# Strassen's block product for the gate and up tiles of two SwiGLU layers

## The chip, the cores and the metric

The kernel runs on one core of one Trainium2 chip, as one program from the inputs in DRAM to the output in DRAM. The metric is the time of one execution in microseconds (us) on the device, the median of several runs. A core has these engines: TensorE (PE, with its weight loads shown apart as PEld), VectorE (DVE), ScalarE (ACT), GpSimd (POOL), and SyncE (SP), which here only issues DMAs.

## What is computed

Two transformer blocks on 512 tokens of width 1024. The first block has two layers: a gated delta rule or a forgetting attention as mixer, and after each mixer a SwiGLU feed-forward layer (FFN) with normed input and normed output:

```python
D_FF = 2816          # of width 1024: 22 tiles of 128

def swiglu(h, w_in, w_out):
    gu = h @ w_in
    return (jax.nn.silu(gu[..., :D_FF]) * gu[..., D_FF:]) @ w_out

for layer in range(2):
    ...                                   # mix: gated delta rule (0), forgetting attention (1)
    x = x + rms_norm(mix, post_mix_norm[layer])
    f = swiglu(rms_norm(x, pre_ffn_norm[layer]), w_ffn_in[layer], w_ffn_out[layer])
    x = x + rms_norm(f, post_ffn_norm[layer])
```

A second block with two other attentions follows. All of it is float32 in the reference, and the output must come close to float32.

## The kernel before

Activations lie transposed: 8 tiles of 128 features by 512 tokens. To keep close to float32, every operand of a big product is split into two float32r parts, `hi` (the rounded value) and `lo` (the rest), and a product of 128x128 weights by a stretch of tokens is three matmuls, hi·hi, hi·lo and lo·hi (`mm3`, L670). A unit of weights (`weight`, L686) is 128 x 1024, that is 8 blocks of 128x128: SP loads it from DRAM, ACT or DVE rounds it into `hi`, ACT or DVE writes `-hi` into `lo`, and a second DMA, issued by POOL, adds the DRAM values onto that (`lows`, L676).

There are five stages: gdn, ffn0, fox, ffn1, b2. An FFN (`ffn`, L883) has 22 pairs of a gate tile and an up tile. In `fm_phase` (L720) each tile of 128 output features is 8 blocks x 3 = 24 matmuls of 512 tokens into one PSUM bank. `evac_in` (L892) takes it out: DVE multiplies by the row norm `y.rb`, ACT and DVE form the SiLU of the gate, DVE or POOL multiplies the two, and the result is split into `hidden[j]`. `FF_CUT` cuts the 22 pairs into stretches of 7, 8 and 7: after each stretch the 8 output tiles are multiplied over its hidden tiles and added up in `f`. At the head of an FFN four tiles, and at its tail four output tiles, are done in two halves of 256 tokens (`HALVES`), so that the norm of one half of the tokens can run beside matmuls of the other. The norm and residual (`add_normed`, L787) come at the end of each mixer and each FFN, nearly all of it on DVE and ACT.

The order of all instructions is made beforehand by a planner (`Program.schedule`, L330). It goes through the recorded operations with a cost for each (`cost`, L258), five queues (PE, DVE, ACT, POOL, SP), and a priority that is the place in the program plus a shift (`SHIFTS`, `later`). Operations that several engines can do (`copy`: ACT or DVE; `tt`: DVE or POOL) go where they end first after a handicap (`DEAR`). `WINDOWS` bounds how far ahead it looks, `QUOTAS` how many weight tiles may be in use at once: 3 raw ones, 10 `hi` or `lo` parts. There are 57 `big` tiles (128 x 512), 21 `wide` ones (128 x 1024) and 8 PSUM banks. A list of engines whose operations exclude each other at a shared port is part of the plan (`locks`, L292). `x`, the residual, stays in 8 `big` tiles through an FFN.

Of the kernel before, what the change touches and what calls it, by code (L numbers as in the profile page):

```python
# [30 lines left out]
DEAR = {"gdn": {"DVE": 650, "ACT": 0, "POOL": 600},  # L31
        "ffn0": {"DVE": 800, "ACT": 0, "POOL": 1000},
        "fox": {"DVE": 850, "ACT": 150, "POOL": 750},
        "ffn1": {"DVE": 450, "ACT": 200, "POOL": 1000},
        "b2": {"DVE": 450, "ACT": -200, "POOL": 400}}
WINDOWS = {"gdn": 881, "ffn0": 1155, "fox": 774, "ffn1": 1400, "b2": 1181}
GDN_ORDER = ("K2 K0 K3 K1 P2 I0 P0 K4 D0 R0 D1 P1 R1 D3 P3 R3 D2 K5 K7 K6 I1 R2 P5 O0 D4 D5 D6 "
             "D7 P7 P4 P6 R4 R6 R5 R7")
FOX_ORDER = "K012 K4 V0 K6 H1 H2 K3 H3 H0 V1 K7 H4 K5 H6 H7 H5 O"
B2_ORDER = "B1 S3 B3 B2 S2 B0 S1 v k q o A1 A0 A2 A3"  # L40
SELECT_SHIFT = 943
START_SHIFT = 50
# [10 lines left out]
class View:  # L53
# [3 lines left out]
    def __init__(self, tile, dt, a, steps=()):  # L57
        self.tile, self.dt, self.a, self.steps = tile, dt, a, steps
# [5 lines left out]
    def __getitem__(self, key):  # L64
        return View(self.tile, self.dt, self.a[key], self.steps + (lambda r: r[key],))
# [475 lines left out]
                getattr(eng[o.eng], fn)(*(real(a) for a in args), **{k: real(a) for k, a in kw.items()})  # L541


class Normed:


    def __init__(self, net):
# [8 lines left out]
class Net:  # L556
# [277 lines left out]

    def out_proj(self, w, o, f, x, post, pre, dst):

        y = Normed(self)
        ws = sum((self.weight_pair(w, m, slice(512, 1024)) for m in range(0, KD, 2)), [])
        for cols in HALVES:
            acc = self.t(256)  # L840
            for m in range(KD):
                bank = self.bank()[:, :256]
                self.fm_tile(bank, ws[m], o, cols)
                self.V.tensor_add(f[m][:, cols], bank, f[m][:, cols])
                self.acc_sq(m, f[m][:, cols], acc)
            self.add_normed(cols, x, f, acc, post, y, pre, dst)
        return y
# [32 lines left out]
            self.block2(first("b2", "n2"), src)  # L880


    def ffn(self, layer, y, x, post, pre, dst):  # L883
        V, A, P = self.V, self.A, self.P
        w_in, w_out = self.d[f"w_ffn_in{layer}"], self.d[f"w_ffn_out{layer}"]
        f = [self.t() for _ in range(KD)]
        nxt = Normed(self)
# [1 line left out]
        gates = {}  # L889
        hidden = {}  # L890

        def evac_in(m, ps, cols):  # L892
            j, up = divmod(m, 2)
            w = cols.stop - cols.start
            if not up:
                gr, th = self.t(w), self.t(w)
                V.tensor_mul(gr, ps, y.rb[:, cols])
                A.activation(th, gr, AF.Tanh, scale=0.5)
                V.scalar_tensor_tensor(gr, th, 1.0, gr, op0=OP.add, op1=OP.mult)
                gates[j, cols.start] = gr  # L900
            else:
                gr = gates.pop((j, cols.start))
                ur = self.t(w)
                V.tensor_mul(ur, ps, y.rb[:, cols])
                self.tt(ur, gr, ur, OP.mult)
                if j not in hidden:
                    hidden[j] = self.t(T, F32R), self.t(T, F32R)
                self.split(hidden[j][0][:, cols], hidden[j][1][:, cols], ur, 0.5)

        j0 = 0  # L910
        for c, n in enumerate(FF_CUT):
            last = c == len(FF_CUT) - 1
            items = [(m, w_in[m]) for m in range(2 * j0, 2 * (j0 + n))]
            self.fm_phase(items, 1024, y.pairs(), evac_in, head=(c == 0))

            def evac_out(m, ps, cols):
                fm = f[m][:, cols]
# [12 lines left out]
            items = [(m, w_out[m][:, j0 * 128:(j0 + n) * 128]) for m in range(KD)]  # L930
# [425 lines left out]
    def fox(self, y, x, w_out):  # L1356
# [89 lines left out]

        for step in FOX_ORDER.split():
            if step[0] == "K":
# [424 lines left out]
```

## Time and profile before

| | us |
|---|---|
| median of 3 runs (1697.17 to 1701.31) | 1697.29 |
| the profiled execution, its own time | 1699.14 |
| its span, from the first to the last instruction | 1697.4 |
| PE busy in the span | 1660.2 |
| DVE, ACT, POOL busy in the span | 1043.3, 916.4, 425.2 |

The profile is of one execution. Busy time of PE is modelled, since matmuls overlap: the distance between starts in a long run of like matmuls tells its pace better than the duration of one (about 400 ns for 512 columns, where starts are some 230 ns apart). A few matmul records can be missing. "Idle before, releaser" says what ended an engine's idle time. All program instructions have line 541 (L541), the line in which the planned order is issued, so groups are told apart by tiles: `big<-psum,big` writes a big tile from a PSUM bank and a big tile, `wide` are weights, `s` small ones.

### The profile page before, as it was taken

The numbers are of one execution on the slowest core, as the hardware profiler recorded it, in microseconds if no ns is written. First come the engines' busy times: TensorE is split into PE (matmuls) and PEld (weight loads), VectorE is DVE, ScalarE is ACT, GpSimd is POOL, SyncE is SP. The second block draws the span as 40 slices with busy tenths as digits, with TensorE's granted clock in tenths as the row PEclk, the third lists the DMA queues.
The fourth block names the chain that finished last, engine by engine and source line by source line (L and its number), as shares of the span: only waits on it lengthen the run. The fifth ranks groups of instructions, "written<-read, shape, count | busy, mean of one in ns | idle before, by whom it ended". The sixth has DMA issues, their size and how long they took to land.

```text
span 1697.4 us, 24959 instructions
## 1 busy us (share of the span) xinstructions
PE 1660.2 (98%) x8886; PEld 1405.1 (83%) x8886; DVE 1043.3 (61%) x2607; ACT 916.4 (54%) x1847; POOL 425.2 (25%) x466
## 2 busy tenths in 40 slices
PE   7999999999999999999999999999999999999999
PEld 5888988997888888887888897888888889898787
DVE  7995875683313223385879684324324477999896
ACT  7643844564234524365978572122512377796694
POOL 3322423221201211122232221201311121413751
PEclk9999999999999999999999999999999999999999
DMA  9746568449967967667354659968958595538723
GB/s 264 161 100 175 101 143 209 119 123 223 214 163 187 222 163 176 158 190 196 88 113 114 161 133 220 229 171 192 231 144 185 132 233 147 126 64 216 170 69 87
DMA packets 105084, 276.24 MB, mean 163 GB/s; under 512 B 24160, under 2 KB 29024, under 8 KB 104960
## 3 DMA queue, kind: packets, MB, share of 16 engines
q0 software_dynamic: 37952, 124.83, 41.0%
q1 hardware_dynamic: 67008, 149.82, 25.7%
q8 instruction: 70, 1.15, 0.3%
q14 instruction: 54, 0.44, 0.1%
HBM read 266.68 MB, written 7.86 MB: 162 GB/s over the span
## 4 chain that ended last, share of the span: by engine, by line
PE 84%; DMA 6%; DVE 4%; issue 3%; POOL 2%; ACT 2%; SPq 0%; POOLq 0%; DVEq 0%; ACTq 0%
PE psum L541 84%; DVE big L541 3%; DMA wide<-in_w_ffn_in_dram 2%; DMA wide<-in_w_gdn_dram 1%; ACT big L541 1%; POOL big L541 1%; DMA wide<-in_gdn_w_out_dram 1%; DMA wide<-in_w_sm_dram 1%; DMA wide<-in_w_v_dram 1%; POOL s L541 1%; ACT wide L541 0%; POOL wide L541 0%; DMA big<-in_xT_dram 0%; DVE wide L541 0%; DMA s<-in_w_ba_dram 0%
## 5 line engine op out<-in xcount | busy, mean ns | idle before, releaser
L541 PE MATMUL psum<-big,wide 128*128 128x512 f32 (+1 forms) x5872 | 1279.8, 372 | 20.5 <-DMA wide<-in_w_gdn_dram 7.3
L541 PEld LDWEIGHTS psum<-big,wide 128*128 128x128 f32 x5872 | 1003.4, 189 | 212.6 <-DMA wide<-in_w_gdn_dram 8.4
L541 DVE TENSOR_TENSOR big<-psum,big 128x512 f32<-128x512 f32 (+5 forms) x334 | 186.4, 566 | 410.0 <-PE psum L541 390.1
L541 ACT ACTIVATE big<-big 128x256 f32<-128x256 f32 (+4 forms) x312 | 159.6, 524 | 458.8 <-DVE big L541 446.1
L541 PE MATMUL psum<-wide,big 128*128 128x512 f32 (+2 forms) x924 | 211.2, 374 | 1.8 <-DMA wide<-in_w_sm_dram 0.8
L541 ACT ACTIVATE wide<-wide 128x1024 fp32r<-128x1024 f32 (+4 forms) x180 | 181.8, 1031 | 23.6 <-PE psum L541 21.6
L541 PEld LDWEIGHTS psum<-wide,big 128*128 128x128 f32 x924 | 156.9, 188 | 29.4 <-DMA wide<-in_w_sm_dram 1.3
L541 POOL DMA_DIRECT2D wide<-in_w_ffn_in_dram x88 | 82.3, 987 | 388.7 <-ACT wide L541 339.2
L541 ACT CAST wide<-wide 128x1024 fp32r<-128x1024 f32 (+3 forms) x178 | 177.0, 1019 | 3.9 <-DMA wide<-in_gdn_w_out_dram 2.1
L541 DVE TENSOR_TENSOR big<-big,big 128x256 f32<-128x256 f32 (+3 forms) x315 | 161.9, 528 | 21.5 <-ACT big L541 17.4
L541 ACT COPY big<-psum 128x512 f32<-128x512 f32 (+3 forms) x128 | 71.7, 560 | 136.4 <-PE psum L541 134.8
L541 DVE SCALAR_TENSOR_TENSOR big<-big,big 128x512 f32<-128x512 f32 (+3 forms) x153 | 103.3, 678 | 65.7 <-ACT big L541 63.5
L541 ACT ACTIVATE big<-big,s 128x128 f32<-128x128 f32 (+3 forms) x266 | 135.5, 542 | 13.0 <-DVE s L541 11.9
L541 PE MATMUL psum<-big,big 128*128 128x128 f32 (+9 forms) x672 | 118.2, 303 | 2.3 <-ACT big L541 1.6
L541 POOL TENSOR_TENSOR s<-s,half 128x4 f32<-128x4 f32 (+2 forms) x50 | 63.4, 1295 | 202.7 <-DVE s L541 191.1
L541 PEld LDWEIGHTS psum<-big,big 128*128 128x128 f32 (+2 forms) x672 | 95.0, 190 | 8.9 <-issue 2.0
L541 PE MATMUL psum<-ident,big 128*128 128x128 f32 (+1 forms) x564 | 94.4, 272 | 4.8 <-DVE big L541 2.8
L541 POOL TENSOR_TENSOR big<-big,big 64x512 fp32r<-64x512 f32 (+3 forms) x56 | 69.8, 1257 | 112.6 <-DVE big L541 41.3
L541 POOL DMA_DIRECT2D wide<-in_w_ffn_out_dram x48 | 44.1, 1045 | 181.2 <-ACT wide L541 149.9
L541 PEld LDWEIGHTS psum<-ident,big 128*128 128x128 f32 (+1 forms) x564 | 68.9, 140 | 20.4 <-issue 4.3
L541 DVE SCALAR_TENSOR_TENSOR big<-big,gains,big 128x256 f32<-128x256 f32 (+2 forms) x144 | 71.8, 525 | 0.7 <-ACT big L541 0.6
L541 DVE CUSTOM_DVE_ANT_0 big<-psum,big 128x384 f32<-128x384 f32 (+3 forms) x120 | 57.3, 495 | 3.3 <-PE psum L541 2.8
(137 smaller groups left out, 1311.6 us busy)
## 6 DMA issues: line engine op xcount, KB each, us to landing
wide<-in_w_ffn_in_dram SPq DMA_DIRECT2D x88, 512.0 KB, 8.2
wide<-in_w_ffn_in_dram POOLq DMA_DIRECT2D x88, 512.0 KB, 9.0
wide<-in_w_gdn_dram SPq DMA_DIRECT2D x31, 512.0 KB, 5.4
wide<-in_w_gdn_dram POOLq DMA_DIRECT2D x31, 512.0 KB, 7.1
wide<-in_w_ffn_out_dram SPq DMA_DIRECT2D x32, 448.0 KB, 5.1
wide<-in_w_ffn_out_dram POOLq DMA_DIRECT2D x32, 448.0 KB, 7.8
wide<-in_w_ffn_out_dram SPq DMA_DIRECT2D x16, 512.0 KB, 7.1
wide<-in_w_ffn_out_dram POOLq DMA_DIRECT2D x16, 512.0 KB, 9.0
```

What stands on the lines that cost most here:

```text
L541: getattr(eng[o.eng], fn)(*(real(a) for a in args), **{k: real(a) for k, a in kw.items()})
```

## The change

In each FFN, 20 of 22 pairs (all but the first two) are no longer two tiles of 24 matmuls over 512 tokens. The gate and up tile over all 1024 input features are taken as a 2 x 2 block matrix (gate and up by the first and the second half of the features), the activations as another (halves of the features by halves of the tokens), and the 2 x 2 product is formed by seven products of halves where the plain way has eight. Each of the seven is 4 blocks x 3 = 12 matmuls of 256 tokens. For that, sums and differences of weight halves are formed and split per pair (`S1` to `S4`), and of the activations once per FFN (`T1` to `T4`, in `seven`, from `x` times the gain). The results are put together with additions out of PSUM. `x` is stored to DRAM (`spare`) once the sums are formed, and loaded again for the end of the FFN. Only three quarters of the weights now take the second DMA (`lows`); the parts of the sums are formed by a subtraction. The 22 pairs are cut differently (6, 6, 5, 5 in four stretches), more weight tiles may be in use (6 raw, 14 parts), the parts of `y` are laid so that halves of them come free early (`Halved`), and the planner's settings for all five stages are others.

```diff
-FF_CUT = (7, 8, 7)
-SHIFTS = {"gdn": 138, "ffn0": 291, "fox": 94, "ffn1": 100, "b2": 226}
+FF_CUT = (6, 6, 5, 5)
+SHIFTS = {"gdn": 157, "ffn0": 291, "fox": 112, "ffn1": 98, "b2": 212}
...
-MARGIN, LATE, SLOW = 50, 1200, 1.04
+MARGIN, LATE, SLOW = 100, 400, 1.02
...
-QUOTAS = {"raw": 3, "parts": 10}
+QUOTAS = {"raw": 6, "parts": 14}
...
+        if halved:
+            for part in (self.hi, self.lo):
+                for k in (0, 2):
+                    a, b = part[k], part[k + 1]
+                    part[k] = Halved(a[:, HALVES[0]], b[:, HALVES[0]])
+                    part[k + 1] = Halved(a[:, HALVES[1]], b[:, HALVES[1]])
...
+    def seven(self, y, x, gain):
...
+        for k in range(4):
+            a, b = self.t(), self.t()
+            self.copy(a, x[k], self.gain(gain, k))
+            self.copy(b, x[k + 4], self.gain(gain, k + 4))
+            lo, hi = HALVES
+            st = []
+            s, t = self.t(), self.t()
+            self.tt(s[:, lo], a[:, hi], a[:, lo], OP.subtract)
+            self.tt(s[:, hi], b[:, hi], s[:, lo], OP.subtract)
+            self.tt(t[:, lo], b[:, hi], a[:, hi], OP.subtract)
+            self.tt(t[:, hi], b[:, lo], s[:, hi], OP.subtract)
+            for u in (s, t):
+                parts = self.t(T, F32R), self.t(T, F32R)
+                self.split(*parts, u)
...
+    def pair_product(self, wg, wu, xs, rb, gated, hi, lo):
...
+        self.load(g, wg)
+        self.load(u, wu)
...
+        self.tt(s[:, a], u[:, a], u[:, b], OP.add)
+        self.tt(s[:, b], s[:, a], g[:, a], OP.subtract)
+        self.tt(t[:, a], g[:, a], u[:, a], OP.subtract)
+        self.tt(t[:, b], g[:, b], s[:, b], OP.subtract)
...
+        self.copy(gp[0], g)
+        self.lows(gp[1], gp[0], g, wg)
+        self.split(*sp, s)
+        self.split(*tp, t)
+        self.copy(both[:, a], u[:, b])
+        self.lows(both[:, b], both[:, a], u[:, b], wu[:, b])
...
+        def product(w, x):
+            out = self.bank()[:, :256]
+            with self.later(self.shift):
+                for k in range(4):
+                    c = slice(k * 128, k * 128 + 128)
+                    self.mm3(out, (lhs[w][0][:, c], lhs[w][1][:, c]), xs[x][k], k == 0, k == 3)
+            return out
...
+        self.copy(p[:, lo_], product("A11", "11"))
+        V.tensor_add(p[:, hi_], product("S2", "T2"), p[:, lo_])
+        V.tensor_add(gr[:, lo_], product("A12", "21"), p[:, lo_])
+        V.tensor_add(q[:, lo_], product("S1", "T1"), p[:, hi_])
+        V.tensor_add(gr[:, hi_], product("S4", "22"), q[:, lo_])
+        self.tt(gr, gr, rb, OP.mult)
+        gated(gr, FULL)
+        last = product("S3", "T3")
+        V.tensor_add(ur[:, hi_], last, q[:, lo_])
+        V.tensor_add(q[:, hi_], last, p[:, hi_])
+        V.tensor_add(ur[:, lo_], product("A22", "T4"), q[:, hi_])
+        self.tt(ur, ur, rb, OP.mult)
+        self.tt(ur, gr, ur, OP.mult)
+        self.split(hi, lo, ur, 0.5)
...
+            plain = 2 if c == 0 else 0
+            if c == 0:
...
+                with self.later(SUMS_SHIFT):
+                    xs = self.seven(y, x, gain)
+                    for m in range(KD):
+                        self.load(spare[m], x[m])
+            for j in range(j0 + plain, j0 + n):
+                hidden[j] = self.t(T, F32R), self.t(T, F32R)
+                self.pair_product(w_in[2 * j], w_in[2 * j + 1], xs, y.rb, gated, *hidden[j])
+            if last:
+                with self.after(hidden[j0][0]):
+                    x = self.loaded(spare)
```

## Rows read from the trace of the kernel before

**Rows 1.** Page, part 1: busy us, share of the span, instructions of each engine.

```profile
PE 1660.2 (98%) x8886; PEld 1405.1 (83%) x8886; DVE 1043.3 (61%) x2607; ACT 916.4 (54%) x1847; POOL 425.2 (25%) x466
```

**Rows 2.** Windows in ffn0: stretch, length, busy PE, PEld, DVE, ACT, POOL; clock, DMA share, GB/s.

```profile
390.00:450.00 60.00, 60.00 (x252) 48.42 (x253) 21.31 (x33) 21.75 (x28) 12.32 (x13) 0.97 0.88 201
450.00:500.00 50.00, 50.00 (x217) 40.47 (x216) 10.10 (x15) 11.09 (x15) 6.66 (x7) 1.00 0.77 192
550.00:600.00 50.00, 50.00 (x217) 40.49 (x216) 10.38 (x15) 25.87 (x28) 11.02 (x13) 1.00 0.93 224
```

**Rows 3.** Waits of PE in the whole span: us in total, times, longest.

```profile
PE psum L541 <- ACT big L541: 7.9, 5, 3.5
PE psum L541 <- DVE big L541: 6.1, 6, 2.3
PE psum L541 <- DMA wide<-in_w_ffn_in_dram: 5.2, 4, 2.7
```

**Rows 4.** Timeline of PE: start, length of the run, matmuls; ffn0 middle, ffn0 tail, ffn1 head.

```profile
449.68 30.59 PE L541 MATMUL psum<-big,wide 128*128 128x512 f32 x131
...
711.83 9.88 PE L541 MATMUL psum<-big,wide 128*128 128x256 f32 x82
...
998.99 13.58 PE L541 MATMUL psum<-big,wide 128*128 128x256 f32 x110
```

**Rows 5.** Groups by shape, DVE: count, busy us, mean ns of one, idle before.

```profile
L541 DVE TENSOR_TENSOR big<-psum,big 128x512 f32<-128x512 f32 x165 | 113.2, 689 | 372.7 <-PE psum L541 372.1
...
L541 DVE TENSOR_TENSOR big<-big,big 128x512 f32<-128x512 f32 x85 | 59.0, 695 | 1.7
L541 DVE SCALAR_TENSOR_TENSOR big<-big,big 128x512 f32<-128x512 f32 x80 | 57.6, 721 | 32.6 <-ACT big L541 30.5 <-PE psum L541 1.8
...
L541 DVE TENSOR_TENSOR big<-psum,big 128x256 f32<-128x256 f32 x70 | 27.7, 417 | 24.7 <-PE psum L541 18.0 <-ACT big L541 6.4
...
L541 DVE TENSOR_TENSOR wide<-wide,wide 128x1024 fp32r<-128x1024 f32 x5 | 6.1, 1218 | 0.5 <-DVE s L541 0.3 <-issue 0.2
```

**Rows 6.** Timeline of DVE: three additions out of PSUM, one behind the other.

```profile
335.64 1.07 DVE L541 TENSOR_TENSOR big<-psum,big 128x256 f32<-128x256 f32 x3
```

**Rows 7.** Groups by shape, ACT, then POOL.

```profile
L541 ACT ACTIVATE wide<-wide 128x1024 fp32r<-128x1024 f32 x151 | 156.1, 1053 | 23.5 <-PE psum L541 21.6 <-issue 1.1
L541 ACT CAST wide<-wide 128x1024 fp32r<-128x1024 f32 x148 | 150.8, 1041 | 2.6 <-DMA wide<-in_gdn_w_out_dram 2.1 <-PE psum L541 0.4
...
L541 POOL TENSOR_TENSOR big<-big,big 128x512 f32<-128x512 f32 x10 | 13.7, 1375 | 17.7 <-DVE big L541 17.6
...
L541 POOL TENSOR_TENSOR wide<-wide,wide 128x1024 fp32r<-128x1024 f32 x3 | 7.5, 2501 | 2.6 <-PE psum L541 2.6
```

**Rows 8.** Page, parts 3 and 6: DMA queues; loads of `w_ffn_in`, us to landing.

```profile
q0 software_dynamic: 37952, 124.83, 41.0%
q1 hardware_dynamic: 67008, 149.82, 25.7%
...
wide<-in_w_ffn_in_dram SPq DMA_DIRECT2D x88, 512.0 KB, 8.2
```

**Rows 9.** Timeline at the end of ffn0: DVE, POOL and PE.

```profile
732.89 3.17 DVE L541 SCALAR_TENSOR_TENSOR big<-big,gains,big 128x256 fp32r<-128x256 f32 x1
733.08 2.69 POOL L541 TENSOR_TENSOR wide<-wide,wide 128x1024 fp32r<-128x1024 f32 x1
...
736.11 1.84 PE L541 MATMUL psum<-big,wide 128*128 128x256 f32 x13 [2.26 <-DVE big L541]
```

**Rows 10.** Head of ffn0: a window (columns as in rows 2), then PE's timeline.

```profile
367.00:377.00 10.00, 10.00 (x81) 9.87 (x82) 10.00 (x29) 6.25 (x16) 0.00 (x0) 1.00 0.00 0
...
382.54 4.66 PE L541 MATMUL psum<-big,wide 128*128 128x512 f32 x19
389.94 10.44 PE L541 MATMUL psum<-big,wide 128*128 128x512 f32 x37 [2.75 <-DMA wide<-in_w_ffn_in_dram]
```

**Rows 11.** Weight loads of PE by shape: count, busy us, mean ns of one.

```profile
L541 PEld LDWEIGHTS psum<-big,wide 128*128 128x128 f32 x5872 | 1003.4, 189 | 212.6 <-DMA wide<-in_w_gdn_dram 8.4 <-DMA wide<-in_w_ffn_in_dram 6.4 <-ACT big L541 5.7
```

More of the change, by code (lines that the diff above doesn't have):

```diff
@@ L28 @@
 HEADS = ((slice(0, 64), slice(64, 128)), (slice(64, 128), slice(0, 64)))
[L29 to L36 removed]
+FF_CUT = (6, 6, 5, 5)
+SHIFTS = {"gdn": 157, "ffn0": 291, "fox": 112, "ffn1": 98, "b2": 212}
+DEAR = {"gdn": {"DVE": 850, "ACT": 200, "POOL": 600},
+        "ffn0": {"DVE": 850, "ACT": -400, "POOL": 1250},
+        "fox": {"DVE": 950, "ACT": 250, "POOL": 800},
+        "ffn1": {"DVE": 1050, "ACT": 100, "POOL": 1050},
+        "b2": {"DVE": 50, "ACT": -200, "POOL": 200}}
+WINDOWS = {"gdn": 881, "ffn0": 869, "fox": 828, "ffn1": 1435, "b2": 839}
 GDN_ORDER = ("K2 K0 K3 K1 P2 I0 P0 K4 D0 R0 D1 P1 R1 D3 P3 R3 D2 K5 K7 K6 I1 R2 P5 O0 D4 D5 D6 "
              "D7 P7 P4 P6 R4 R6 R5 R7")
[L39 to L42, printed above, removed]
+FOX_ORDER = "K012 K4 V0 K6 H1 H2 K3 H3 H0 V1 K5 K7 H4 H6 H7 H5 O"
+B2_ORDER = "B1 B3 S3 B2 S2 B0 S1 v k q o A1 A0 A2 A3"
+SELECT_SHIFT = 1129
+SUMS_SHIFT = 33
+START_SHIFT = 107
 CLOCK = 3413.0
 NEAR = {"gdn": 0.0, "ffn0": 0.0, "fox": 0.25, "ffn1": 0.0, "b2": 0.0}
[L45 removed]
+MARGIN, LATE, SLOW = 100, 400, 1.02
 FIRST_KEYS = (-2, 7.5)
 KINDS = {"psum": (8, 512), "big": (57, 512), "wide": (21, 1024), "s128": (6, 128), "s64": (12, 64), "s8": (32, 8)}
[L48 removed]
+QUOTAS = {"raw": 6, "parts": 14}
 GAINS = ("pre0", "post0", "pref0", "postf0", "pre1", "post1", "pref1", "postf1", "kv", "n2")
@@ L880, in run @@
             self.block2(first("b2", "n2"), src)
+    def seven(self, y, x, gain):
+        sums = []
+        for k in range(4):
[12 more added lines that the diff above has]
+                self.split(*parts, u)
+                st += [(parts[0][:, c], parts[1][:, c]) for c in HALVES]
+            sums.append(st)
+        pair = lambda k, c: (y.hi[k][:, c], y.lo[k][:, c])
+        out = {"11": [pair(k, HALVES[0]) for k in range(4)], "21": [pair(k + 4, HALVES[0]) for k in range(4)],
+               "22": [pair(k + 4, HALVES[1]) for k in range(4)]}
+        out.update({f"T{i + 1}": [sums[k][i] for k in range(4)] for i in range(4)})
+        return out
@@ new lines, in pair_product @@
+    def pair_product(self, wg, wu, xs, rb, gated, hi, lo):
+        V = self.V
+        g, u = (self.g.tile("wide", 1024, quota="raw") for _ in range(2))
+        self.load(g, wg)
+        self.load(u, wu)
+        part = lambda n=1024: tuple(self.g.tile("wide", n, F32R, quota="parts") for _ in range(2))
+        a, b = slice(0, 512), slice(512, 1024)
+        s, t = (self.g.tile("wide", 1024, quota="raw") for _ in range(2))
+        self.tt(s[:, a], u[:, a], u[:, b], OP.add)
+        self.tt(s[:, b], s[:, a], g[:, a], OP.subtract)
+        self.tt(t[:, a], g[:, a], u[:, a], OP.subtract)
+        self.tt(t[:, b], g[:, b], s[:, b], OP.subtract)
+        gp, sp, tp = part(), part(), part()
+        both = self.g.tile("wide", 1024, F32R, quota="parts")
+        self.copy(gp[0], g)
[4 more added lines that the diff above has]
+        self.lows(both[:, b], both[:, a], u[:, b], wu[:, b])
+        half = lambda p, c: (p[0][:, c], p[1][:, c])
+        lhs = {"A11": half(gp, a), "A12": half(gp, b), "A22": (both[:, a], both[:, b]),
+               "S1": half(sp, a), "S2": half(sp, b), "S3": half(tp, a), "S4": half(tp, b)}
+        def product(w, x):
[4 more added lines that the diff above has]
+                    self.mm3(out, (lhs[w][0][:, c], lhs[w][1][:, c]), xs[x][k], k == 0, k == 3)
+            return out
+        lo_, hi_ = HALVES
+        p, q, gr, ur = self.t(), self.t(), self.t(), self.t()
+        self.copy(p[:, lo_], product("A11", "11"))
[12 more added lines that the diff above has]
+        self.split(hi, lo, ur, 0.5)
@@ L912, in ffn @@
             last = c == len(FF_CUT) - 1
-            items = [(m, w_in[m]) for m in range(2 * j0, 2 * (j0 + n))]
-            self.fm_phase(items, 1024, y.pairs(), evac_in, head=(c == 0))
+            plain = 2 if c == 0 else 0
+            if c == 0:
+                items = [(m, w_in[m]) for m in range(2 * plain)]
+                self.fm_phase(items, 1024, y.pairs(), evac_in, head=True)
+                with self.later(SUMS_SHIFT):
[8 more added lines that the diff above has]
+                    x = self.loaded(spare)
             def evac_out(m, ps, cols):
```

21 lines of the change are left out of this document (15 added, 6 removed).

## The prediction

> **What bounds the kernel now.** I read first the busy times of the page [rows 1]: PE 1660.2 of 1697.4 us, so it stands idle for 37 us in all, and no other engine is above 61%. A modelled PE can look busy without being at its pace, so next come the windows of the FFN [rows 2]: in ffn0's middle PE is busy for 50.00 of 50.00 us, with 217 matmuls of 512 columns in each window, while DVE and ACT run for 10 to 26 us. The waits of PE [rows 3] show what little there is: 5.2 us for FFN weights, 7.9 for ACT, 6.1 for DVE, in the whole span. So PE's own work is what the FFNs cost: work taken from it shortens them, until another engine is late.
>
> **PE's work.** The runs of like matmuls give the pace [rows 4]. 512 columns: (30.59 − 0.40) / 130 = 0.232 us from start to start. 256 columns: (9.88 − 0.28) / 81 = 0.1185 us at ffn0's tail; (13.58 − 0.28) / 109 = 0.122 us at ffn1's head, where a stall or a missing record may be in it. (0.40 and 0.28 are the modelled length of the last matmul.) A pair was 2 tiles x 8 blocks x 3 = 48 matmuls, 48 x 0.232 = 11.15 us. It becomes 7 products x 4 blocks x 3 = 84 narrow ones, 84 x 0.1185 = 9.95 us. That saves 1.19 us in each of 40 pairs (20 in each FFN): **−47.7 us**. The bounds are 84 x 0.122 (−36 us) and exactly half the wide pace, 0.116 (−56 us). I take 0.1185, since that run stands in the same loop over the same kinds of tiles with all its operands there. Two plain pairs and the output product stay: the new cut changes no count of matmuls.
>
> **The work on the vector engines per pair.** It about doubles, and is the price of the change. DVE or POOL must do: 4 additions of 512 weight columns, 2 subtractions of 1024 (the `lo` of both sums), 3 products of 512 (twice the row norm, gate times up); DVE alone: 7 additions of 256 out of PSUM, 2 scalar-tensor operations of 512. With the durations of [rows 5] this is 4 x 0.695 + 2 x 1.218 + 3 x 0.695 + 7 x 0.417 + 2 x 0.72 = 11.66 us in 18 instructions. Records of consecutive ones overlap: three additions of 0.417 fill 1.07 us [rows 6], which is 0.33 from one to the next, 0.09 less than one lasts. So 18 of them in close order are 11.66 − 1.6 = 10.1 us of DVE, if POOL takes none. ACT has four copies of 1024 (g twice, the two sums), two of 512, three small ones, some 4 x 1.05 [rows 7] + 2.7 = 6.9 us, and is not the limit. Before, DVE's part of a pair was two products out of PSUM, a product and two scalar-tensor operations of 512, 2 x 0.689 + 0.695 + 2 x 0.72 = 3.5 us.
>
> 10.1 us of DVE stands against 9.95 us of PE. Two things make it fit. After each stretch of pairs comes the output product, 8 x 18 x 0.232 = 33 us of PE for 6 pairs, in which DVE has 8 additions (5.5 us; in [rows 2] it is busy 10 of 50 us there). With 14 parts allowed and 7 to a pair, one pair's weights can be prepared in it (4 x 0.605 + 2 x 1.13 = 4.7 us). So a stretch of six needs 6 x 10.1 − 4.7 = 56 of its 59.7 us: 94%. And POOL, which in these stretches issues only DMAs, may take some, at twice the time (1.375 for 512, 2.501 for 1024 [rows 7]). Eight PSUM banks hold 8 x 1.42 = 11 us of narrow products, so a late addition need not stop PE.
>
> **Transfers.** From the queues' shares [rows 8] the adding queue moves 124.83 MB in 41.0% of 1697.4 us, 179 GB/s, the plain one 149.82 MB in 25.7%, 343 GB/s. The adding DMA is spared a quarter of a pair's weights, 0.26 MB, 1.5 us, 29 us per FFN; storing and reloading `x` adds 4.2 MB, 12 us, in an FFN of over 340. So the DMA engines have less to do. The stores join SP's queue when `x` is final and hold nothing behind them; the reload waits for tiles of the sums to come free, and the output weights of the last stretch are queued behind it. I put it at nothing, since six raw tiles may be loaded ahead; if that cover is gone, one load's 8.2 us [rows 8] is due per FFN.
>
> **What becomes late.** Three places, each costed from a row.
> - In the pairs, at 94%, DVE and POOL will meet. [Rows 9] show what it costs: POOL subtracts 1024 columns (2.69 us), a DVE operation begun just before takes 3.17 us where its like takes 0.5, and PE waits 2.26 us. Bounds: nothing, or one in each pair (90 us). I take two per FFN that reach PE, since the banks hold 11 us: +9.0 us.
> - At the head. DVE is full up to 377 [rows 10], 10.00 of 10.00 us. Then it owes the sums of the activations (16 x 0.33 + 8 x 0.605 = 10.1 us), the weights of the first pair (4.7) and what is left of the head's gates (some 12 x 0.33 = 4): ready at 396 if DVE does all. PE is through with the head's tiles at 382.5 [rows 10] and has three products in each pair that need no sum; two pairs' worth is 6 x 1.42 = 8.5 us, to 391. The stall lies between 0 (POOL takes half) and 13.5 us; one of 2.75 us stands there already, and behind it the clock was granted at 0.97 over 60 us [rows 2], for a while at the lower of its two levels, 1.2 GHz, after PE had stood idle: 1.8 us. I take +2.5 net for each FFN: +5.0 us.
> - At the tail. The second half of the last four output tiles covers the norm of the first. It shrinks with the last stretch from 7 to 5 hidden tiles, 4 x 3 x 2 = 24 matmuls, 2.8 us. ffn0's tail has already a wait on DVE [rows 9]; behind ffn1 other products stand ready. Bounds 0 and 5.6; I take +2.8 us.
>
> More weight tiles at once should give back half of PE's 5.2 us of waits for FFN weights [rows 3]: −2.6 us (bounds 0 and −5.2). The new settings of the other stages can go either way, by about the size of PE's largest waits in [rows 3], 7 us; I take 0.
>
> **The sum.** −47.7 + 9.0 + 5.0 + 2.8 − 2.6 = −33.5 us. The profiled execution took 1699.14 us (1697.4 of span and 1.7 around it), 1.85 above the median of 1697.29. 1699.14 − 33.5 = 1665.6, less 1.85: **1664 us**.
>
> **Rivals.**
> - *All of it is hidden.* The plan spreads DVE's work so that no wait is added: 1697.3 − 47.7 − 2.6 = 1647. For it: PE without a gap through ffn0's middle [rows 2]. Against it: 94% of DVE, where there was less than half before. Chance 0.18.
> - *DVE sets the pace of the pairs.* If the steps wait for one another (each addition out of PSUM needs the one before), DVE goes between 10.1 and 11.66 us per pair; halfway, 10.9, leaves 0.25 us x 40 = 10 us of gain, and with head and tail some 1692. For it: the chain of the seven additions. Against: 33 us in each stretch in which to catch up. What decides is whether DVE is busy all through a stretch of pairs. Chance 0.17.
> - *The shared port: slower than before.* Its place is the pairs, its price [rows 9], where POOL's operation and a DVE operation exclude each other. DVE's operations with two inputs in SBUF take 4 x 0.605 + 2 x 1.13 + 3 x 0.605 + 2 x 0.63 = 7.8 us of a pair. With both 1024-wide subtractions moved to POOL the two engines hold it 5.5 + 5.0 = 10.5 us, with one addition more 11.3, with two 12.0. So from the third operation of a pair on POOL the kernel is slower than before; at four it is 0.9 x 40 = 36 us, and with head and tail 1741. Against: the planner knows the exclusion, and holds POOL back by a handicap. Chance 0.07. The Trainium skill ("SBUF — State Buffer", Who interferes with whom) says that DVE instructions with two SBUF inputs and GpSimd instructions that read SBUF block each other whole, whoever is first; [rows 9] bear that out for one pair of instructions.
> - *Weight loads pace the narrow matmuls: slower.* Each of the 84 needs its own load, where 48 did, and a load lasts 0.189 us in the records [rows 11]. If it could not overlap, a pair would be 84 x 0.189 = 15.9 us, 190 us more in all: some 1890. Against: 81 steps of 0.1185 us with a load in each [rows 4]. Chance 0.02. The Trainium skill ("TensorE: Matmul & The Clock Gate", Back-to-back issue gap) has a rule that speaks against the change: the spacing is set by load and matmul together, 81 ns at 128 columns and 131 ns at 512. A straight line between them gives an estimate of 98 ns at 256, where two narrow ones cost 1.5 times a wide one, and the change would lose 77 us. The trace differs, 118.5 against 232 ns, a factor of 1.02 for two, and the measurement decides.
>
> **How the numbers follow.** The forecast has 0.56: a wait or two at each of its places. With *hidden* (0.18) and 0.12 of *DVE's pace* that makes 0.86 faster; 0.05 of *DVE's pace* lies within 0.3% (5 us, about what a measurement of this kernel can tell from no change); port and loads make 0.09 slower. The range is 1641 to 1692: below 1641 no sum reaches but with the narrow pace at its lower bound; above lie the two slower rivals and the end of *DVE's pace*, 0.14.
>
> **What would show it.** Right: runs of 84 narrow matmuls some 0.1185 us apart; PE busy some 45 us less over the span; DVE over 80% in the pairs' stretches and low in the output products; the adding queue at 114 MB, 40 x 0.26 = 10.5 MB less. Wrong, by step: PE idle well above 37 + 14 us, with waits on DVE within the pairs (DVE's pace) or on operations of 3 us beside POOL (port); spacing of 0.13 and more (loads); a gap of over 5 us between the head's tiles and the first narrow products (sums); SP's loads late in the last stretch (reload).

## The result and the profile after

The changed kernel takes 1654.22 us (median of four runs, 1651.64 to 1655.54) against 1697.23 before: 43.0 us less, a ratio of 0.974 (95% interval 0.9719 to 0.976). The forecast was 1664 with a range of 1641 to 1692. The profiled execution took 1651.64 us with a span of 1649.9, 47.5 less than the profiled one of before.

The first line of the page and the largest waits of PE answer to [rows 1, 3]:

```profile
PE 1617.8 (98%) x10278; PEld 1443.7 (88%) x10278; DVE 1321.1 (80%) x3118; ACT 1043.1 (63%) x2055; POOL 510.1 (31%) x531
```

```profile
PE psum L542 <- DVE big L542: 9.5, 10, 2.9
PE psum L542 <- ACT big L542: 6.5, 5, 3.6
...
PE psum L542 <- DMA wide<-in_w_ffn_in_dram: 0.7, 1, 0.7
```

PE is busy 42.4 us less and idle about as long (32 us, 37 before). DVE rose by 278 us without PE's idle time rising. Waits for FFN weights nearly vanished (5.2 before). Windows of ffn0's head and then of its middle (stretch, length, busy PE, PEld, DVE, ACT, POOL; clock, DMA share, GB/s), answer to [rows 2, 10]:

```profile
384.00:404.00 20.00, 16.36 (x110) 15.74 (x109) 18.20 (x41) 13.01 (x23) 5.75 (x7) 0.83 0.43 93
...
480.00:500.00 20.00, 20.00 (x172) 20.00 (x171) 18.08 (x33) 14.24 (x20) 7.39 (x7) 1.00 0.93 199
...
540.00:560.00 20.00, 20.00 (x109) 17.12 (x107) 11.08 (x16) 6.93 (x9) 1.73 (x2) 1.00 0.57 133
...
580.00:600.00 20.00, 20.00 (x172) 20.00 (x171) 16.93 (x31) 11.78 (x19) 4.33 (x5) 1.00 0.96 234
...
640.00:660.00 20.00, 20.00 (x172) 20.00 (x171) 18.87 (x34) 12.48 (x18) 7.82 (x9) 1.00 1.01 255
```

In the pairs (480, 580, 640) PE has no gap: 172 matmuls touch each 20 us, (20.00 + 0.28) / 172 = 0.118 us each. DVE is busy for 85 to 94% there, and for 55% in a stretch with output products (540). The one bad window is the head, 384 to 404: PE is busy 16.36 of 20 us and the granted clock is 0.83 on average, so part of it was at the lower level, 1.2 GHz, after PE had stood idle. The same columns for both FFNs from behind the head to near the end, then ffn1's head and its first pairs:

```profile
404.00:704.00 300.00, 300.00 (x2088) 279.09 (x2088) 226.01 (x383) 165.73 (x233) 87.10 (x88) 1.00 0.87 205
1004.00:1304.00 300.00, 300.00 (x2084) 278.85 (x2083) 232.80 (x382) 168.92 (x236) 104.39 (x105) 1.00 0.85 204
```

```profile
984.00:1004.00 20.00, 18.69 (x150) 17.84 (x149) 19.61 (x46) 15.59 (x32) 6.39 (x8) 1.00 0.73 174
1004.00:1024.00 20.00, 20.00 (x169) 19.87 (x168) 19.96 (x37) 13.39 (x20) 8.49 (x8) 1.00 0.62 158
```

So PE shows no idle time in 300 us of either FFN, and DVE is closer to its bound in places than the three windows of ffn0 tell: in ffn1's first pairs it is busy for 19.96 of 20.00 us. ffn1's head has a smaller gap, 1.31 of 20 us, and there the clock stays at 1.00.

To see where the time went, I cut the span at one event that comes once in each mixer and FFN: the column sums over the first half of the tokens at its end, four matmuls with `ones`. In PE's timeline they are, first before, then after, then in an experiment told of below (`no_product`: all of the change but the block product):

```profile
342.40 0.50 PE L541 MATMUL psum<-ones,big 128*128 128x1 f32 x4
721.55 0.50 PE L541 MATMUL psum<-ones,big 128*128 128x1 f32 x4
976.13 0.50 PE L541 MATMUL psum<-ones,big 128*128 128x1 f32 x4
1353.02 0.50 PE L541 MATMUL psum<-ones,big 128*128 128x1 f32 x4
```

```profile
345.69 0.50 PE L542 MATMUL psum<-ones,big 128*128 128x1 f32 x4
705.25 0.50 PE L542 MATMUL psum<-ones,big 128*128 128x1 f32 x4
952.36 0.50 PE L542 MATMUL psum<-ones,big 128*128 128x1 f32 x4
1310.14 0.50 PE L542 MATMUL psum<-ones,big 128*128 128x1 f32 x4
```

```profile
345.69 0.50 PE L542 MATMUL psum<-ones,big 128*128 128x1 f32 x4
723.30 0.50 PE L542 MATMUL psum<-ones,big 128*128 128x1 f32 x4
970.56 0.50 PE L542 MATMUL psum<-ones,big 128*128 128x1 f32 x4
1347.10 0.50 PE L542 MATMUL psum<-ones,big 128*128 128x1 f32 x4
```

The differences, in us (the last column runs to the end of the span), with other experiments taken in the same way:

| kernel | gdn | ffn0 | fox | ffn1 | b2 | span |
|---|---|---|---|---|---|---|
| before | 342.4 | 379.2 | 254.6 | 376.9 | 344.4 | 1697.4 |
| after | 345.7 | 359.6 | 247.1 | 357.8 | 339.8 | 1649.9 |
| no_product | 345.7 | 377.6 | 247.3 | 376.5 | 339.8 | 1686.9 |
| one_ffn | 345.1 | 377.6 | 247.2 | 358.5 | 340.0 | 1668.4 |
| other_settings | 346.2 | 377.2 | 256.5 | 377.4 | 349.1 | 1706.4 |
| old_margins | 371.1 | 357.7 | 249.2 | 365.3 | 349.2 | 1692.4 |

The two FFNs gave 19.6 and 19.1 us. Fox and b2, which the product does not touch, gave 7.5 and 4.6, and gdn lost 3.3. The shorter tail moves 24 narrow matmuls (2.8 us) from behind each mark to ahead of it, so of the gains of fox and b2 5.6 belong to the FFNs. A single profile has its own scatter: in six runs told of below that keep the order of instructions of the changed kernel and alter nothing in gdn, gdn took 345.7 to 350.8 us.

### The profile page after: what moved, and what is told of

It reads as the page before. It is cut to its first block, busy times and chain, and to the rows that moved or that the text cites. A ratio compares the mean times of both kernels' runs of the same rounds, so it can differ in the third digit from the quotient of the medians.

```text
span 1649.9 us, 29036 instructions
## 1 busy us (share of the span) xinstructions
PE 1617.8 (98%) x10278; PEld 1443.7 (88%) x10278; DVE 1321.1 (80%) x3118; ACT 1043.1 (63%) x2055; POOL 510.1 (31%) x531
## 3 DMA queue, kind: packets, MB, share of 16 engines
q0 software_dynamic: 40256, 114.34, 39.2%
## 4 chain that ended last, share of the span: by engine, by line
PE 84%; DVE 7%; DMA 4%; ACT 3%; issue 1%; POOL 0%; SPq 0%; DVEq 0%; ACTq 0%
PE psum L542 84%; DVE big L542 5%; ACT big L542 2%; DMA wide<-in_w_gdn_dram 2%; DVE wide L542 1%; DVE s L542 1%; ACT wide L542 1%; DMA wide<-in_w_ffn_in_dram 1%; DMA wide<-in_gdn_w_out_dram 1%; DMA wide<-scratch_blocks_a 0%; ACT s L542 0%; DMA scratch_x<-big 0%; DMA scratch_blocks_a<-big 0%; DMA scratch_spare<-big 0%; POOL s L542 0%
## 5 line engine op out<-in xcount | busy, mean ns | idle before, releaser
L542 PE MATMUL psum<-big,wide 128*128 128x256 f32 (+2 forms) x7264 | 1231.2, 326 | 16.9 <-DVE big L542 5.4
L542 PEld LDWEIGHTS psum<-big,wide 128*128 128x128 f32 x7264 | 1043.1, 189 | 128.4 <-DVE big L542 8.2
L542 DVE TENSOR_TENSOR big<-psum,big 128x256 f32<-128x256 f32 (+5 forms) x550 | 252.7, 475 | 111.1 <-PE psum L542 96.7
L542 ACT CAST wide<-wide 128x1024 fp32r<-128x1024 f32 (+4 forms) x289 | 266.3, 939 | 108.0 <-PE psum L542 53.9
L542 DVE TENSOR_TENSOR big<-big,big 128x256 f32<-128x256 f32 (+3 forms) x434 | 244.0, 576 | 21.4 <-ACT big L542 16.5
L542 ACT ACTIVATE wide<-wide 128x1024 fp32r<-128x1024 f32 (+4 forms) x230 | 208.0, 911 | 45.4 <-PE psum L542 28.7
L542 DVE TENSOR_TENSOR wide<-wide,wide 128x1024 fp32r<-128x1024 f32 (+1 forms) x174 | 168.1, 976 | 32.0 <-PE psum L542 29.6
L542 ACT COPY big<-psum 128x512 f32<-128x512 f32 (+3 forms) x162 | 82.1, 511 | 123.5 <-PE psum L542 119.5
L542 ACT ACTIVATE big<-big,s 128x128 f32<-128x128 f32 (+3 forms) x259 | 132.3, 545 | 10.7 <-DVE s L542 10.5
L542 POOL DMA_DIRECT2D wide<-in_w_ffn_out_dram x64 | 56.5, 906 | 145.7 <-ACT wide L542 102.1
L542 POOL TENSOR_TENSOR wide<-wide,wide 128x512 f32<-128x512 f32 (+1 forms) x34 | 61.2, 1820 | 49.4 <-ACT big L542 13.5
```

## The experiments

Two theories are set against each other. *PE's work*: the gain is the matmul time saved in the pairs, DVE's added work lies beside it and just fits, and what is lost is lost at the heads. *Settings*: a good part of the gain comes from the planner's settings, margins and quotas, which changed with it. Further runs put a larger dose on single costs: DVE, POOL, the sums, the round trip of `x`. Where "in its own order" is said, the planned order of instructions is that of the changed kernel, and only the named instructions are repeated or put on another engine.

**One FFN alone.**

```diff
+            plain = n if layer == 0 else 2 if c == 0 else 0
+            if layer == 0:
+                items = [(m, w_in[m]) for m in range(2 * j0, 2 * (j0 + n))]
+                self.fm_phase(items, 1024, y.pairs(), evac_in, head=(c == 0))
...
-            if last:
+            if last and layer == 1:
```

> The block product in ffn1 alone; ffn0 multiplies all its pairs in the plain way, in the same four stretches, with x left in its tiles; all settings as in the changed kernel. Theory 'PE's work': each FFN's gain is its own 20 x 1.2 us of matmul time, so half of it is lost: 1654 + 22 to 24 = 1676 to 1678 us. Rival 'the settings': a good part of the 43 us comes from the planner's settings and the larger quotas, which stay: 1654 to 1665.

Measured: 1670.43 us (ratio 0.9839, 0.9824 to 0.9854), 16.2 above the changed kernel. Less than the 22 to 24 expected, but the loss lies where it should: in the table ffn0 goes back from 359.6 to 377.6, and no other stage moves by more than 0.7. So the product is worth 16 to 18 us in an FFN, not the 24 of its matmul time; a quarter to a third is lost again within the FFN.

**The settings without the product.** After that the settings could be priced: plain pairs in both FFNs, all else as after.

```diff
-        y = Normed(self, halved=True)
+        y = Normed(self)
...
-            for j in range(j0 + plain, j0 + n):
-                hidden[j] = self.t(T, F32R), self.t(T, F32R)
-                self.pair_product(w_in[2 * j], w_in[2 * j + 1], xs, y.rb, gated, *hidden[j])
+            items = [(m, w_in[m]) for m in range(2 * j0, 2 * (j0 + n))]
+            self.fm_phase(items, 1024, y.pairs(), evac_in, head=(c == 0))
```

> The changed kernel with all pairs of both FFNs multiplied in the plain way, x left in its tiles, no sums; the cut in four stretches, the quotas, the margins and all other settings as in the changed kernel. Theory 'PE's work, less the head': the product is worth in each FFN what one_ffn lost, 16 us, so 1654 + 32 = 1686 us, and what is left of the 43 us, 11, belongs to quotas, margins and settings together. Rival 'only the product gives': 1697 or more.

Measured: 1688.19 us (ratio to before 0.9951, 0.9934 to 0.9968). As expected, to 2 us. The block product with its sums, its splits and the round trip of `x` is worth 34.0 us; quotas, margins, cut and settings together are worth 8.5. In the table fox and b2 are as short without the product as with it. But 2.8 us of each of these gains is the tail's shift, and counted with its FFN the gains are 4.4 us in ffn0, 3.2 in ffn1, 4.5 in fox and 1.8 in b2, with 3.3 lost in gdn: so most of it comes inside the FFNs, where PE no longer waits for their weights (5.2 us before).

Against this run the place of the product's loss can be read too. The stretch from an FFN's mark to its first matmul of 512 columns (the columns of windows as above), first after, then no_product, ffn0 and ffn1 in each:

```profile
345.69:417.74 72.05, 66.78 (x531) 65.54 (x530) 67.47 (x159) 49.28 (x97) 17.93 (x20) 0.95 0.61 140
952.36:1022.76 70.40, 67.79 (x546) 65.23 (x545) 67.38 (x158) 51.45 (x99) 21.49 (x22) 1.00 0.57 141
```

```profile
345.69:371.30 25.61, 24.06 (x200) 23.60 (x199) 22.63 (x65) 18.68 (x39) 7.25 (x9) 1.00 0.73 161
970.56:995.95 25.39, 23.97 (x200) 23.52 (x199) 21.86 (x63) 19.37 (x41) 6.44 (x8) 1.00 0.68 156
```

Of the matmuls 505, 520, 180 and 180 have 256 columns (the counts in the lines take in some 20 small ones, and two begun before); at 0.118 us that is 59.6, 61.4, 21.2 and 21.2 us. What goes beyond is 12.5 and 9.0 us after, 4.4 and 4.2 in no_product: the heads with the product lose some 8 us more in ffn0 and some 5 in ffn1. In ffn0 it is idle time (5.3 us against 1.6) and clock (0.95 on average over the 72 us, some 3.4 us). In ffn1 idle time is only 1.2 us more and the clock is full; the rest does not show as idle time. A matmul's record of 0.28 us hides a stall of up to 0.16 us at this pace.

**Parts of the settings.** First the other stages' settings put into the kernel before, then the old margins put into the changed kernel.

```diff
-SHIFTS = {"gdn": 138, "ffn0": 291, "fox": 94, "ffn1": 100, "b2": 226}
+SHIFTS = {"gdn": 157, "ffn0": 291, "fox": 112, "ffn1": 100, "b2": 212}
...
-SELECT_SHIFT = 943
-START_SHIFT = 50
+SELECT_SHIFT = 1129
+START_SHIFT = 107
```

> The kernel before, with the changed kernel's settings of gdn, fox and b2 (shifts, handicaps, windows, the orders of fox and b2, the two shifts of b2 and of the start); the FFNs' settings, quotas and margins are the old ones. Theory 'settings give': fox and b2 gain some 5 and 2 us, gdn loses 3: 1690 to 1694. Rival 'settings fit only the plan that they were made with': no gain, 1697, or slower by up to 1% (1714).

Measured: 1708.3 us (ratio 1.0062, 1.0042 to 1.0081): slower. Fox and b2 gain nothing (256.5, 349.1). The rival holds: in the kernel before, with its margins, quotas and pairs, these settings give nothing.

```diff
-MARGIN, LATE, SLOW = 100, 400, 1.02
+MARGIN, LATE, SLOW = 50, 1200, 1.04
```

> The changed kernel with the old margins of the planner (50, 1200 and 1.04 instead of 100, 400 and 1.02: the plan counts on data to land 0.8 us later and on engines 2% slower). Theory 'the margins are part of the change': a plan that counts on later data and slower engines leaves PE with gaps when DVE stands at 90% in the pairs: 1665 to 1690. Rival 'the product alone': 1654, within 4 us.

Measured: 1695.72 us (ratio to before 0.9989, 0.9979 to 1.0), 41.5 above the changed kernel. With three numbers of the planner put back, the whole gain is gone, where 1665 to 1690 was expected, and not in the way that I had thought: the table shows ffn0 at 357.7, as good as with the new margins, ffn1 7.5 us longer, b2 9.4, and gdn, in which no operation was changed, 25 us longer. In gdn PE waits 10.2 us for DVE and 12.0 for ACT (3.8 and 4.9 after), and the granted clock over the first 340 us is 0.97 on average (1.00 after). So ffn0 keeps the product's gain, and the plan made with these numbers loses as much elsewhere. That it is because the settings no longer fit together is an argument; which of the three numbers does it stays open.

**Narrowness alone.** The kernel before, pairs 2 to 21 in halves of 256 tokens, with eight products for eight.

```diff
+                    if narrow(m) and cols == FULL:
+                        for c in HALVES:
+                            self.fm_tile(bank[:, c], w, xs, c)
+                    else:
+                        self.fm_tile(bank, w, xs, cols)
```

> The kernel before, with all matmuls of pairs 2 to 21 done in two halves of 256 tokens (eight products of halves, 96 narrow matmuls for 48 wide ones, no sums). It measures the price of narrowness alone. Theory 'narrow at 0.118 us': 40 x (96 x 0.118 - 48 x 0.232) = +8 us, 1705. Rival 'weight loads pace them' at 0.13 and more: +54 us or more, 1751.

Measured: 1710.38 us (ratio 1.0073, 1.0058 to 1.0089), 12.8 more, where 8 were expected and 54 by the rival. PE's timeline gives the pace in the middle of ffn0, and its waits a part of the rest:

```profile
499.72 52.55 PE L541 MATMUL psum<-big,wide 128*128 128x256 f32 x442
```

```profile
PE psum L541 <- DMA wide<-in_w_ffn_in_dram: 9.2, 3, 5.6
```

(52.55 − 0.28) / 441 = 0.1185 us, the forecast's figure, with a weight load for each. By the marks the two FFNs take 385.7 and 385.0 us, 14.7 more than before, and the other stages 3.4 less. What exceeds 8 there is partly the waits for FFN weights, from 5.2 to 9.2 us, and partly the clock: over the span it was granted at 0.995 against 0.999, some 7 us. PE's idle time in all did not grow (36.6 us, 37.2 before).

**More work for DVE.** In the changed kernel's own order, two of the four additions of a pair, then all four, issued twice:

```diff
-                getattr(eng[o.eng], fn)(*(real(a) for a in args), **{k: real(a) for k, a in kw.items()})
+                for _ in range(2 if o.tag == "add" else 1):
+                    getattr(eng[o.eng], fn)(*(real(a) for a in args), **{k: real(a) for k, a in kw.items()})
```

> The changed kernel in its own order of instructions, with two of the four additions of weight halves per pair (the first of S and its follower) issued twice, one behind the other: 2 x 0.6 to 0.7 us more of DVE in each pair (more where POOL has them), 40 pairs. In the windows of pairs DVE is busy some 17 to 18 of 20 us, 8.7 us of a pair's 9.93, so this takes it to the bound. Theory 'DVE just fits': 0 to +12 us (1654 to 1666). Rival 'DVE already sets the pace': each added us counts, 40 x 1.25 = +50 us. Rival 'DVE has room': 0.

> As two_adds_twice, with all four additions issued twice: 2.5 to 2.8 us more of DVE per pair, 11.3 against PE's 9.93. Theory 'DVE just fits': over the bound by some 1.3 us in each pair, less what the output products' stretches take up: +25 to +55 us (1680 to 1709). Rival 'DVE has room': under +10 us.

Measured: 1687.25 us (ratio to before 0.9934, 0.9917 to 0.9952) and 1727.81 (1.0173, 1.0158 to 1.0188), that is 33 and 74 us above the changed kernel. The first dose was expected to cost at most 12, the second at most 55. By the marks DVE is busy in the two FFNs for 53 us more with the first dose and 109 with the second, which cost 33 and 74: on average two thirds of each added microsecond. The FFNs differ. With the first dose ffn0 becomes 9.3 us longer and ffn1 21.7, with the second 30.6 and 41.1. Part of the cost is the clock, granted at 0.993 and 0.984 over the span against 0.998 after, up to 8 and 24 us. PE's waits and the windows of two_adds_twice:

```profile
PE psum L545 <- ACT big L545: 20.5, 10, 3.9
PE psum L545 <- DVE big L545: 13.0, 15, 3.0
```

```profile
480.00:500.00 20.00, 20.00 (x171) 20.00 (x170) 19.42 (x34) 11.85 (x17) 6.19 (x6) 1.00 0.72 149
...
560.00:580.00 20.00, 20.00 (x157) 19.36 (x156) 14.09 (x22) 8.01 (x12) 6.12 (x5) 1.00 0.68 158
```

In the first of these windows, all pairs, DVE is at 97%. PE is full in both; its new waits, elsewhere, are for DVE and for ACT, whose tanh and last copy in a pair come behind DVE's products; the longest for ACT (up to 3.6 us) stand before the output products, which need the last pair. So the changed kernel lies close to the point from which DVE sets the pace, ffn1 closer than ffn0. The order is fixed, so that DVE cannot use its idle time of the output products' stretch for pairs that come later; whether an order planned anew would take the added work better, no run shows.

**POOL's part.** The pairs' operations that the plan had put on POOL (16 of 512 and 1024 columns in the middle of ffn0) issued on DVE; then the reverse, both 1024-wide subtractions of every pair on POOL.

```diff
+                by = "DVE" if o.tag == "tt" and o.eng == "POOL" else o.eng
+                fn, args, kw, _ = o.ways[by]
...
```

> The changed kernel in its own order, with the pairs' tensor operations that the plan gave to POOL (16 to 18 in each FFN) issued on DVE at the same place. Theory 'the port costs nothing where the plan put POOL': 1654, within 4 us. Rival 'the port': POOL's operations held DVE up, the kernel gains 5 us or more.

Measured: 1653.9 us (ratio 0.9739, 0.9723 to 0.9755), no change. By the pages' counts it moves 42 operations in both FFNs, heads and tails included (DVE x3118 to x3160, POOL x531 to x489). DVE's busy time rose by 9 us (1330.4 against 1321.1), so a little more work on DVE, spread as here, still cost nothing.

```diff
+                by = "POOL" if o.tag == "low" and "POOL" in o.ways else o.eng
+                fn, args, kw, _ = o.ways[by]
...
```

> The changed kernel in its own order, with both 1024-wide subtractions of each pair on POOL. Theory 'the port is exclusive and POOL takes twice as long': the port is held 5.5 + 4.9 = 10.4 us of a pair's 9.93, and POOL's adding DMAs stand behind the subtractions: +15 to +60 us (1669 to 1714). Rival 'no exclusion': DVE is relieved of 2.3 us a pair, 1654 or faster.

Measured: 1732.42 us (ratio 1.0199, 1.0181 to 1.0217), 78 us more than the changed kernel and slower than before, beyond the 15 to 60 expected. The groups by shape, DVE in ffn0's middle (398 to 690), first after, then in this run, show how (count, busy us, mean ns):

```profile
L542 DVE TENSOR_TENSOR big<-psum,big 128x256 f32<-128x256 f32 x138 | 55.1, 417 | 23.1 <-PE psum L542 21.4 <-DVE big L542 0.5
...
L542 DVE TENSOR_TENSOR big<-big,big 128x512 f32<-128x512 f32 x60 | 42.1, 704 | 1.1
...
L542 DVE SCALAR_TENSOR_TENSOR big<-big,big 128x512 f32<-128x512 f32 x20 | 16.1, 807 | 0.5 <-ACT big L542 0.5
```

```profile
L545 DVE TENSOR_TENSOR big<-big,big 128x512 f32<-128x512 f32 x50 | 64.5, 1291 | 1.0
L545 DVE TENSOR_TENSOR big<-psum,big 128x256 f32<-128x256 f32 x117 | 46.3, 417 | 11.6 <-PE psum L545 9.8
...
L545 DVE SCALAR_TENSOR_TENSOR big<-big,big 128x512 f32<-128x512 f32 x17 | 28.4, 1672 | 5.8 <-ACT big L545 5.7
```

Two groups of DVE operations with two inputs in SBUF go from 704 to 1291 ns and from 807 to 1672, as they would if they stood behind POOL's; those that read PSUM stay at 417. Other groups with two inputs in SBUF rise less (696 to 788, 685 to 764), so the loss is not the same for all of them. The Trainium skill ("SBUF — State Buffer", Who interferes with whom) says that DVE instructions with two SBUF inputs contend with GpSimd (POOL) instructions that read SBUF, and that those with at most one, outside its two-port modes, do not. Here the trace agrees on the middle of a whole stage. The port is not all of the 78 us: PE also waits 9.8 us for weight parts that POOL itself writes late, and the clock was granted at 0.983 over the span (0.998 after), up to 26 us. The run doesn't part them further.

**The sums at the head.** Every instruction that forms T1 to T4 issued twice, in the changed kernel's own order; then none of them issued, the products taking halves of `y` instead (planned anew; the sums of activations are left out).

```diff
+                for _ in range(2 if o.tag == "sums" else 1):
...
```

> The changed kernel in its own order, with every instruction that forms T1 to T4 (16 subtractions of 256, 8 scaled copies, 8 splits in each FFN) issued twice, one behind the other: some 10 us more of DVE or POOL and 10 us of ACT at each FFN's head. Theory 'the sums stand on the path at the head': +8 to +20 us for both FFNs (1662 to 1674). Rival 'the sums are hidden beside the head's tiles': within 3 us of 1654.

```diff
-        sums = []
...
-        out.update({f"T{i + 1}": [sums[k][i] for k in range(4)] for i in range(4)})
+        for i, (j, c) in enumerate(((0, 0), (4, 0), (4, 1), (4, 1))):
+            out[f"T{i + 1}"] = [pair(k + j, HALVES[c]) for k in range(4)]
```

> The changed kernel without the work of forming T1 to T4: the products take halves of y in their place, so the sums of activations are left out (and the 16 tiles that held them); all other work, the round trip of x too, and all settings stay; the order is planned anew. Theory 'what the product lost, it lost to the sums at the head' (matmul time saved 48 us, product worth 34 to 37, so 11 to 14 lost): 1654 - 8 to 14 = 1640 to 1646 us, and no slow clock behind the head of ffn0. Rival 'the loss lies in the pairs or in the round trip': 1650 or more.

Measured: 1691.34 us with the sums formed twice (ratio to before 0.9969, 0.9958 to 0.9979), 37 us more than after, and 1652.14 without them (0.9733, 0.9717 to 0.9749), only 2 less. Both miss: the doubling was expected to cost 8 to 20, and the removal to give 8 to 14, so that by its number the rival of no_sums came true. The doubling says that work at this place stands on the path in both FFNs (by the marks 17.1 and 20.2 us longer), and that delays there grow: DVE is busy for 14.8 us more in each, and the clock was granted at 0.991 (0.998 after), up to 12 us in all. The removal disagrees at first sight. The heads of no_sums, ffn0 and ffn1, in windows, and PE's longest single wait:

```profile
381.00:404.00 23.00, 22.71 (x193) 22.50 (x192) 20.81 (x42) 13.79 (x23) 10.59 (x9) 1.00 0.68 180
984.00:1010.00 26.00, 22.03 (x174) 21.83 (x173) 21.05 (x35) 15.95 (x25) 15.64 (x13) 0.93 0.81 186
```

```profile
PE psum L542 <- ACT wide L542: 4.0, 1, 4.0
```

In ffn0 the head is whole again: PE busy 22.71 of 23.00 us at full clock, where after has 16.36 of 20.00 at 0.83; ffn0 by the marks is 354.4, 5.2 less. In ffn1 another wait takes the place, 4.0 us for weights that ACT prepares, with a clock of 0.93 after it; ffn1 is 360.6, 2.8 more. Counted as above, from the mark to the first matmul of 512 columns, what goes beyond the pace falls in ffn0 from 12.5 to 6.6 us, and rises in ffn1 from 9.0 to 10.4. So in ffn0 most of the head's loss was the sums, as far as a run can show it whose order was planned anew and which has 16 tiles more to use. In ffn1 it stays open whether it is the sums or the preparation of the first pair's weights, since both are ready late at the same place. The gain of 5 us in ffn0 comes to 2 in the whole since ffn1 lost 2.8 and gdn, with no change of its own, 2.0.

**The round trip of x.** Stores and loads issued twice, in the changed kernel's own order.

```diff
+                for _ in range(2 if o.tag == "trip" else 1):
...
```

> The changed kernel in its own order, with the stores of x to DRAM and the loads back issued twice each: 16 more DMAs and 4.2 MB more per FFN. Theory 'the round trip is hidden': 1654, within 4 us. Rival 'SP's queue or the DMA engines are late at the head or in the last stretch': +5 to +16 us (a load's 8.2 us in each FFN).

Measured: 1699.12 us (ratio to before 1.0015, 0.9998 to 1.0032), 45 us more, far beyond both. The doubling brought a wait of its own: the second DMA of each tile does not start before the first has landed, and SP stands at each one, at the reloads and at the stores:

```profile
SPq L545 <- DMA big<-scratch_spare: 60.3, 16, 6.6
SPq L545 <- DMA scratch_spare<-big: 45.0, 16, 5.4
```

SP's timeline in ffn0's last stretch, then PE's, in this run; then SP's after:

```profile
639.97 38.33 SPq L545 DMA_DIRECT2D big<-scratch_spare  x16
678.35 0.42 SPq L545 DMA_DIRECT2D wide<-in_w_ffn_out_dram  x1
```

```profile
684.80 15.39 PE L545 MATMUL psum<-big,wide 128*128 128x256 f32 x105 [13.72 <-DVE wide L545]
```

```profile
637.35 4.87 SPq L542 DMA_DIRECT2D big<-scratch_spare  x8
648.32 0.33 SPq L542 DMA_DIRECT2D wide<-in_w_ffn_out_dram  x1
```

So the run does not price the trip. It shows what the trip needs to stay hidden: SP issues the eight reloads in 4.87 us and is free for the output weights, which are queued behind them. When it stood there for 38 us, these weights were issued 30 us later and PE waited for 13.7. That the reload is hidden in the changed kernel is seen in its own trace, where PE has no idle time up to 704 and 1304; what the stores cost at the head, no run prices.

## Why the prediction was right, and where its terms were off

- **PE's work, −47.7: right.** The pace of 0.1185 us held in the pairs and in narrow_pairs. The rival of the weight loads does not hold here: two narrow matmuls cost 1.02 of a wide one. The estimate of 1.5 from the Trainium skill ("TensorE: Matmul & The Clock Gate", Back-to-back issue gap) does not agree with this trace. One statement was wrong and cost nothing to speak of: the new cut does change the count of matmuls, as the shorter tail turns 48 narrow ones into 24 wide ones in each FFN (10278 − 8886 = 1392 more, not 40 x 36 = 1440).
- **DVE per pair, 10.1 us, 94% of a stretch of six: about right.** From mark to mark DVE is busy for 280.2 and 284.5 us, against 138.5 and 133.0 in no_product. Less some 10 to 15 us for the sums, that is 6.3 to 7.1 us more for each of 20 pairs, where 6.6 was forecast. The windows shown have DVE at 85 to 100% in the pairs. That it *just* fits is shown by two_adds_twice, which cost more than the 12 us that I had expected at most: the banks and the output products take up less than I had counted on.
- **Collisions in the pairs, +9.0: wrong.** There are none that show at PE; it has no idle time in 300 us of either FFN. The plan puts only 16 operations of ffn0's middle on POOL, and moving them to DVE changes nothing. The price was not right either. By the rival's own sum two operations of a pair on POOL hold the port for 10.5 us against 9.95 of PE, 22 us in all, and the kernel is slower than before only from the third operation on; lows_on_pool, with the two subtractions there, cost 78 and was slower than before. That its 1732 us is near the 1741 given for four operations is luck. But the danger was real; the plan did not go there.
- **Head, +5.0: mis-sized.** Matmul time saved is 48 us, the product is worth 34.0 by medians and 37 by the profiled spans, so 11 to 14 us were lost again. The heads account for it: some 8 us in ffn0, where PE is idle for 3.6 us in 20 and loses 3.4 (17% of 20) to the lower clock, which the forecast had taken as unchanged; some 5 in ffn1, at full clock. The place was right and the size was less than half. What is not settled is the share of the sums in ffn1.
- **Tail, +2.8: wrong.** From the mark to the end of the following norm it took 36.0 and 36.4 us before, 32.3 and 33.1 after. It fell by the 2.8 us of matmuls that left it and a little more: no wait came instead, and PE's idle time in it went from 2.3 and 1.5 us to 0.2 and nothing.
- **Waits for weights, −2.6: right in kind,** 5.2 to 0.7 us, and none in no_product, so it belongs to the quotas, margins and settings.
- **The round trip of `x`, nothing: right for the reload,** behind which PE has no idle time in either FFN; the stores were not priced.
- **Settings of the other stages, 0: mis-sized.** Quotas, margins, cut and settings give 8.5 us together. Of this some 3 us come in fox, b2 and gdn together, within the bound of 7 to either side; the rest comes in the FFNs, where only the 2.6 of the weights had been counted.

In sum: 9.0 + 2.8 us of costs that did not come and 6 of gain that was not counted, against 6 to 9 too little at the heads. That is the 10 us between 1664 and 1654. The mechanism of the forecast held: PE's work sets the FFNs' time, DVE just fits, and the price stands at the heads; PE is busy 42.4 us less where 45 was given as a sign, and the adding queue moved 114.34 MB where 114 was. That the time came within 10 us is in part luck, since errors of some 18 and 6 to 9 us ran against each other.

## What to carry to other kernels

Where one engine is full and the others are not, work may be exchanged for theirs, but price it in the stretch where it falls, engine by engine: here 1.2 us of PE per pair was bought with some 6.6 us of DVE, and two_adds_twice shows how near DVE then stood to its bound. Here it cost most where the engine that takes the work over was already full, at the heads, beside the norm. And when an order is planned for the whole program, price the plan apart from the idea: the same product was worth 34 us with one set of the planner's numbers, and with three of them put back the whole gain was gone, 25 of 41 us of it in a stage that the product does not touch.

## What the runs showed of the hardware

- Under a fixed order of instructions, work added to DVE, which was busy for 85 to 100% of the pairs' windows shown, cost on average two thirds of its time (33 us for 53, 74 for 109), lower clock included; with the first dose 9.3 us in one FFN and 21.7 in the other. 9 us, by moving 42 operations of both FFNs from POOL to DVE, cost nothing.
- POOL's subtraction of 1024 columns (2.4 to 2.7 us) holds up DVE operations with two inputs in SBUF, on average over ffn0's middle by 0.1 to 0.9 us each, by their group, and leaves those that read PSUM at their 417 ns.
- Idle time of PE can cost twice: after 3.6 us of it in 20 at ffn0's head, the clock of that window was 0.83 of full speed on average, which is again 3.4 us. After 1.3 us in 20 at ffn1's head the clock stayed at 1.00.
- Two matmuls of 256 columns, each with a weight load of its own, took 1.02 of the time of one of 512 columns (0.1185 us and 0.232 from start to start).
- A DMA that must wait for an earlier one into the same tile holds all of SP's queue: 38 us for 16 issues, where 8 without the wait take 4.87, so some 10 by that pace.
